# Where a mixer's weights are split, and how the last tile and the norm are cut

## The chip, the cores and the metric

The kernel runs on one core of a Trainium2 chip, in one launch. The metric is the device time of that core in microseconds (us), as a median of several executions. The tables come from one execution that the hardware profiler recorded: its own time, its span (first to last instruction) and, within it, every instruction's start and duration. Engines: PE is TensorE, whose weight loads are shown apart as PEld; DVE is VectorE, ACT ScalarE, POOL GpSimd, SP SyncE, which here only issues DMAs. Each engine works its own list in its own order and waits on semaphores.

## The reference, cut to what matters

One encoder layer on 512 tokens of width 1024, in float32:

```python
def swiglu(x, w_gate, w_up, w_down):
    return (jax.nn.silu(x @ w_gate) * (x @ w_up)) @ w_down

x = x + 0.5 * swiglu(rms_norm(x, ffn1_norm), ffn1_w_gate, ffn1_w_up, ffn1_w_down)   # d_ff = 2816
h = rms_norm(x, mix_norm)
qkv_a, z_a, a_a, b_a, qkv_b = split(h @ w_in)          # w_in: 1024 x 3600
o_a = gdn_mixer(qkv_a, z_a, a_a, b_a, conv_w, ...)     # bidirectional gated DeltaNet, 4 heads of 128
o_b = dilated_mixer(qkv_b, q_norm_w, k_norm_w, rel_bias)   # windowed softmax attention, 8 heads of 64
x = x + concatenate([o_a, o_b]) @ w_out
x = x + 0.5 * swiglu(rms_norm(x, ffn2_norm), ffn2_w_gate, ffn2_w_up, ffn2_w_down)
x = rms_norm(x, final_norm)
```

## The kernel before

Activations lie transposed: eight tiles `x[0..7]` of 128 features x 512 tokens. A product in nearly full precision is made of three matmuls in the reduced type fp32r (`mm3`, line 228): every operand is split into a rounded part `hi` (a cast on ACT) and the remainder `lo` (a subtraction on DVE), and PE sums hi x hi, hi x lo and lo x hi. So weights have to be split on the chip before PE can use them, and each tile of 128x128 weights costs three matmuls of 512 columns.

**First SwiGLU block** (`ffn`, line 284, called with `gu1`, `dn1`). For each of 22 slices of d_ff, gate (`pg`) and up (`pu`) are summed over eight k tiles; then eight output tiles `pd` are summed over the 22 slices. Weights of one such sum come by `wload` (line 165): one DMA on SP's queue into `wraw` (two buffers), a cast into `whi` (line 176), a subtraction into `wlo` (line 177).

**Presplit.** In the same block `share` (line 280) calls `presplit` (line 196) 76 times. It loads one 128x512 piece of weights that come later (56 of `w_in`, 16 of `w_out`, 4 of the second block's first slice, listed in `plan`), casts it into `phi` (line 205), subtracts in place (`praw`, line 206), and `send` (line 191) stores both parts to DRAM (`ws`). All these DMAs are on SP's queue, in program order with the block's own loads.

**Mixer.** A generator per piece of work, and `interleave` (line 63), a planner with hand-set due times, fix the program order; a scheduler places instructions on the engines from it. `px` runs the projections in the order of the string `ORDER`: two *units* of weights for each 128 features (a unit is one piece of `plan`, four 128x128 tiles, 12 matmuls). `wnext` (line 213) hands out a unit: it issues the loads of ready-split units from `ws` (512 KB each) up to `AHEAD` = 3 in advance into the pool `w` of four buffers. Beside the projections run four heads' `gram` (line 594: transposes, products, eight scaled products `M` each on DVE, and eight small `D` stores on SP), `solve` (line 814: 122 small operations on DVE), the levels of a triangular inverse, the `scan`, and attention `att`. In this part PE's order is fixed.

**Second SwiGLU block** (`late=True`): as the first, without presplit; its first slice takes four units from `wnext`. Behind the last output tile (d = 7) stands the final norm: `x[7]` is updated in two halves of 256 tokens (line 335), squared, summed over features by a matmul with ones into `pr`, then `rsq` (line 233) makes the inverse root in `R`, and eight products `y` by `R` (line 1237, two of them on POOL) are stored.

Of the kernel before, what the change touches and what calls it, by code (L numbers as in the profile page):

```python
# [35 lines left out]
GIN, VGO, VGV, PRG, NRG, VTG, VBG, OPG, OTG, FNG, SVG, SSD, SST, VTP, LVH = 9.5, 16.5, 4.0, 0.5, 6.0, 3.5, 3.5, 13.5, 0.75, 10.5, 0.75, 8.0, 0.6, 3.0, 1.3  # L36
AHEAD = 3
PRI = 0, 1, 2, 4, 3, 5
# [52 lines left out]
def encoder_layer(ctx, tc, xT, gu1, dn1, win, wab, wo1, wo2, gu2, dn2, cols, relb, masks, onehot, lnc, sel, out):  # L91
# [95 lines left out]
    plan += [gu2[0, j, :, 4 * u:4 * u + 4] for j in range(2) for u in range(2)]  # L187
    ws_d = [dr.tile([P, 2 * T], F32, name=f"ws{i}") for i in range(len(plan))]
    made, raws, unsent = [0], [], []
# [6 lines left out]
    def presplit():  # L196

        i = made[0]
        made[0] += 1
        for n in range(i if i == 0 else i + 1, min(i + 2, len(plan))):  # L200
            raws.append(tmp("xp", "praw", T + 4, bufs=3)[:, 0:T])
            sy.dma_start(out=raws[-1], in_=plan[n].rearrange("p a b -> p (a b)"))
        lo = raws.pop(0)
        hi = WF["pool"].tile([P, T], F32R, tag="phi", name="phi", bufs=2)
        se.copy(hi, lo)  # L205
        ve.tensor_tensor(out=lo.bitcast(F32R), in0=lo, in1=hi.bitcast(F32), op=ALU.subtract)  # L206
        if unsent:
            send()
        unsent.append((i, hi, lo))

    taken, ready = [0], []

    def wnext():
        while taken[0] < len(plan) and len(ready) <= AHEAD:
            t = wp.tile([P, 1024], F32, tag="w", name="wsp", bufs=4)
            sy.dma_start(out=t, in_=ws_d[taken[0]])
            taken[0] += 1
            ready.append([t[:, i * T:(i + 1) * T].bitcast(F32R).rearrange("p (a b) -> p a b", b=P) for i in range(2)])
        return ready.pop(0)

# [58 lines left out]

    def share(step):  # L280
        while made[0] < len(plan) and made[0] * (2 * NF + 3 * NKT - 8) < len(plan) * (step - 3):
            presplit()

    def ffn(gu, dn, norm, nxt, then=None, late=False, mid=None):
        with tc.tile_pool(name="wf", bufs=2, reuse_waits="tile") as wf, \
# [5 lines left out]
            for f in range(NF):  # L291
                pg, pu = palt("pg"), palt("pu")
                for j, pt in ((0, pg), (1, pu)):
# [27 lines left out]
                wait = []  # L321
            for d in range(NKT):
                pd = palt("pd")
                for f0, n in ((0, 8), (8, 8), (16, 6)):
                    wh, wl = wload(dn[d, :, f0:f0 + n], n, P)
                    if not late:
                        share(2 * NF + 3 * d + f0 // 8)
# [3 lines left out]
                    if late and d == NKT - 1 and f0 == 8:  # L331
                        with tc.issue_after(act["mm"].ins):
                            mid()
                for s in (slice(0, 256), slice(256, 512)) if late and d == NKT - 1 else (slice(0, 512),):
                    ve.scalar_tensor_tensor(out=x[d][:, s], in0=pd[:, s], scalar=0.5, in1=x[d][:, s], op0=ALU.mult,
                                            op1=ALU.add)
                nxt(d)
# [19 lines left out]
    ffn(gu1, dn1, n1, after1, bring)  # L357
    while unsent:
        send()
    with tc.issue_after(act["lastf"].ins):  # L360
        sy.dma_start(out=mk, in_=masks)

    with ExitStack() as mctx:
        mp = mctx.enter_context(tc.tile_pool(name="mp", bufs=1, reuse_waits="tile"))
# [856 lines left out]
    hs = [slice(256 * i, 256 * i + 256) for i in range(2)]
    tail = tmp("sq", "tail")
    preload()
    for pr, s in zip(prs, hs):
        se.activation(tail[:, s], x[7][:, s], AF.Square)
        te.matmul(pr[:, 0:256], lhsT=ones, rhs=tail[:, s], start=False, stop=True)
        rsq(R[:, s], pr[:, 0:256], 1024.0, "u")
    ys.append(slot("xh7", "y"))
    for d in range(NKT):
        y = ys[d]  # L1230
        if d == NKT - 1:
            ve.scalar_tensor_tensor(out=y, in0=x[d], scalar=col[:, C_FIN + d:C_FIN + d + 1], in1=R, op0=ALU.mult,
                                    op1=ALU.mult)
            (sy, se)[d % 2].dma_start(out=out[d], in_=y)
        else:
            for s in hs if d == 0 else (slice(0, T),):
                (gp if d in (1, 4) else ve).tensor_tensor(out=y[:, s], in0=y[:, s], in1=R[:, s], op=ALU.mult)  # L1237
                (sy, se)[d % 2].dma_start(out=out[d, :, s], in_=y[:, s])

# [79 lines left out]
```

## Time and profile before

| what | us |
|---|---|
| median of three executions | 1121.74 (1119.83 to 1124.93) |
| the profiled execution, its own time | 1124.95 |
| its span | 1123.2 |
| busy in the span: PE / PEld | 1071.6 / 871.1 |
| busy in the span: DVE / ACT / POOL | 613.1 / 441.1 / 90.3 |
| mean granted TensorE clock | 0.990 |

Busy times are unions of recorded durations. Matmuls are pipelined and their ends are modelled, so a recorded duration (0.39 us for 512 columns) is longer than the distance from one start to the next, and a PE that is busy is not a PE at its peak. An idle time is put down to the semaphore that came last before the waiting instruction.

### The profile page before, as it was taken

Reading aid. Unit: us, or ns where it says so; the run is one execution under the profiler, and the core shown is the slowest. Engines: PE = TensorE matmul, PEld = TensorE weight load, DVE = VectorE, ACT = ScalarE, POOL = GpSimd, SP = SyncE. Lnnn points to the kernel's source line nnn. Section 1 sums busy time; section 2 is a strip of 40 time slices with the busy share of each in tenths; the row PEclk is TensorE's granted clock in tenths of the full one; section 3 lists DMA queues with packets and bytes.
Section 4 is the critical chain, followed back from the end, with each engine's and each line's share of the span. In section 5 each row is a group of like instructions: output and inputs, shape, how many; then the busy total and the mean of one; then the engine's idle time right before and its main releaser. Section 6 shows DMA issues by size and latency. Waiting matters only on the chain. (4 is left out here: it accounts for less than half of the span.)

```text
span 1123.2 us, 14359 instructions
## 1 busy us (share of the span) xinstructions
PE 1071.6 (95%) x5312; PEld 871.1 (78%) x5312; DVE 613.1 (55%) x1108; ACT 441.1 (39%) x812; POOL 90.3 (8%) x121
## 2 busy tenths in 40 slices
PE   8999999999999999999999989999999999999994
PEld 5787777777788868778788867778888888888883
DVE  5655655655443358678566778565444444522223
ACT  6533443444332226422574756344332222322221
POOL 3000000000011123440000020100000000001111
PEclk9999999999999999999999999999999999999997
DMA  7788888988993334676723363352222323323332
GB/s 258 263 267 281 278 290 285 297 279 278 305 306 120 99 117 158 188 229 217 181 86 99 112 212 111 110 191 93 95 94 94 97 97 107 96 86 101 100 88 75
DMA packets 85062, 191.99 MB, mean 171 GB/s; under 512 B 21520, under 2 KB 22320, under 8 KB 84992
## 3 DMA queue, kind: packets, MB, share of 16 engines
q1 hardware_dynamic: 80800, 178.68, 49.7%
q0 software_dynamic: 2896, 10.25, 3.0%
q10 hardware_dynamic: 1296, 2.15, 0.5%
q8 instruction: 41, 0.67, 0.3%
q14 instruction: 29, 0.24, 0.1%
HBM read 142.24 MB, written 48.81 MB: 170 GB/s over the span
## 5 line engine op out<-in xcount | busy, mean ns | idle before, releaser
L176 ACT CAST whi<-wraw 128x1024 fp32r<-128x1024 f32 (+1 forms) x138 | 137.5, 998 | 269.0 <-PE pd L53 91.3
L177 DVE TENSOR_TENSOR wlo<-wraw,whi 128x1024 fp32r<-128x1024 f32 (+1 forms) x138 | 159.9, 1159 | 107.4 <-ACT whi L176 105.2
L53 PE MATMUL pg<-xh,whi 128*128 128x512 f32 x344 | 136.8, 398 | 7.2 <-ACT whi L176 7.2
L53 PE MATMUL pg<-xh,wlo 128*128 128x512 f32 x344 | 136.5, 397 | 6.9 <-DVE wlo L177 6.9
L53 PE MATMUL pd<-hh,whi 128*128 128x512 f32 x352 | 137.9, 392 | 2.6 <-ACT whi L176 2.6
L53 PE MATMUL pu<-xh,wlo 128*128 128x512 f32 x344 | 134.8, 392 | 4.8 <-DVE wlo L177 4.8
L53 PE MATMUL pd<-hh,wlo 128*128 128x512 f32 x352 | 137.7, 391 | 0.0
L53 PE MATMUL pd<-hl,whi 128*128 128x512 f32 x352 | 137.5, 391 | 0.0
L53 PE MATMUL pg<-xl,whi 128*128 128x512 f32 x344 | 135.9, 395 | 0.1
L53 PE MATMUL pu<-xh,whi 128*128 128x512 f32 x344 | 134.1, 390 | 0.0
L53 PE MATMUL pu<-xl,whi 128*128 128x512 f32 x344 | 133.9, 389 | 0.0
L206 DVE TENSOR_TENSOR praw<-praw,phi 128x512 fp32r<-128x512 f32 x76 | 53.4, 706 | 116.1 <-ACT phi L205 116.0
L205 ACT CAST phi<-praw 128x512 fp32r<-128x512 f32 x76 | 47.0, 620 | 155.7 <-DMA praw<-in_win 103.3
L53 PEld LDWEIGHTS pg<-xh,wlo 128*128 128x128 f32 x344 | 65.3, 190 | 24.8 <-DVE wlo L177 11.3
L53 PEld LDWEIGHTS pg<-xh,whi 128*128 128x128 f32 x344 | 65.3, 190 | 22.5 <-ACT whi L176 8.7
L53 PEld LDWEIGHTS pu<-xh,wlo 128*128 128x128 f32 x344 | 64.5, 188 | 21.5 <-DVE wlo L177 8.4
L53 PEld LDWEIGHTS pd<-hh,whi 128*128 128x128 f32 x352 | 66.5, 189 | 16.7 <-ACT whi L176 3.1
L53 PEld LDWEIGHTS pd<-hh,wlo 128*128 128x128 f32 x352 | 66.3, 188 | 14.7 <-DVE wlo L177 0.9
L53 PEld LDWEIGHTS pg<-xl,whi 128*128 128x128 f32 x344 | 65.1, 189 | 16.1 <-DVE xl L269 2.5
L53 PEld LDWEIGHTS pd<-hl,whi 128*128 128x128 f32 x352 | 66.5, 189 | 14.0
L53 PEld LDWEIGHTS pu<-xl,whi 128*128 128x128 f32 x344 | 64.6, 188 | 13.5
L53 PEld LDWEIGHTS pu<-xh,whi 128*128 128x128 f32 x344 | 64.6, 188 | 13.5 <-ACT whi L176 0.3
(292 smaller groups left out, 1626.9 us busy)
## 6 DMA issues: line engine op xcount, KB each, us to landing
wraw<-in_gu SPq DMA_DIRECT2D x84, 512.0 KB, 3.9
wsp<-ws SPq DMA_DIRECT2D x76, 512.0 KB, 3.5
ws<-phi SPq DMA_DIRECT2D x76, 256.0 KB, 3.6
ws<-praw SPq DMA_DIRECT2D x76, 256.0 KB, 4.5
wraw<-in_dn SPq DMA_DIRECT2D x32, 512.0 KB, 3.6
praw<-in_win SPq DMA_DIRECT2D x56, 256.0 KB, 4.2
wraw<-in_dn SPq DMA_DIRECT2D x16, 384.0 KB, 3.2
praw<-in_wo SPq DMA_DIRECT2D x16, 256.0 KB, 4.1
```

Source lines behind the costliest of these rows:

```text
L53: self.last = f(*a, **k)
L176: se.copy(hi[:, s], raw[:, s])
L177: ve.tensor_tensor(out=lo[:, s], in0=raw[:, s], in1=hi.bitcast(F32)[:, s], op=ALU.subtract)
L205: se.copy(hi, lo)
L206: ve.tensor_tensor(out=lo.bitcast(F32R), in0=lo, in1=hi.bitcast(F32), op=ALU.subtract)
```

## The change

- `presplit`, `send`, `share`, the DRAM tiles `ws` and `AHEAD` are gone. The pool of four weight buffers becomes two tags: `wa` with three and `wb` with one; in the SwiGLU blocks `wtile` hands them out in turn.
- `wopen`, at the end of the first block, takes `wb` as one raw tile `wrw` with two halves and issues two loads. `wnext` keeps up to three `wa` tiles, splits every one but the newest (cast on ACT, subtraction on DVE) and issues the raw load two units ahead into the half that the split has just left.
- The last output tile of the second block is made in two halves of 256 tokens: three `wload`s first, then 66 matmuls of 256 columns for each half. `mid(0)` and `mid(1)` put the ones-matmuls, and the whole final norm of the first half (`close(0)`), into the stream of matmuls; `close(1)` follows the second half. All products and stores have 256 columns now.
- Eight matmuls of ones with ones stand first in PE's list.

```diff
-AHEAD = 3
+    pw = pat("warm")
+    for i in range(8):
+        te.matmul(pw[:, 0:P], lhsT=ones, rhs=ones, start=True, stop=True)
...
-            hi, lo = (wp.tile([P, 1024], F32R, tag="w", name=nm, bufs=4) for nm in ("whi", "wlo"))
+            hi, lo = (wtile(nm) for nm in ("whi", "wlo"))
...
-    def send():
-        i, hi, lo = unsent.pop(0)
-        sy.dma_start(out=ws_d[i][:, 0:T], in_=hi.bitcast(F32))
-        sy.dma_start(out=ws_d[i][:, T:2 * T], in_=lo)
...
+    def wtile(name, dt=F32R):
+
+        nw[0] += 1
+        t, n = ("wb", 1) if nw[0] % 4 == 0 else ("wa", 3)
+        return wp.tile([P, 1024], dt, tag=t, name=name, bufs=n)
+
+    def fetch(i):
+        if i < len(plan):
+            r = wraw[0][:, i % 2 * T:(i % 2 + 1) * T]
+            sy.dma_start(out=r, in_=plan[i].rearrange("p a b -> p (a b)"))
+            fetched.append(r)
+
+    def wopen():
+        while nw[0] % 4 != 3:
+            nw[0] += 1
+        wraw.append(wtile("wrw", F32))
+        for i in range(2):
+            fetch(i)
...
     def wnext():
-        while taken[0] < len(plan) and len(ready) <= AHEAD:
-            t = wp.tile([P, 1024], F32, tag="w", name="wsp", bufs=4)
-            sy.dma_start(out=t, in_=ws_d[taken[0]])
...
+        while got[0] < len(plan) and len(ready) < 3:
+            t = wp.tile([P, 1024], F32R, tag="wa", name="wsp", bufs=3)
+            ready.append(t)
+            got[0] += 1
+        while got[1] < got[0] - (got[0] < len(plan)):
+            i = got[1] - got[0] + len(ready)
+            split(ready[i][:, 0:T], ready[i][:, T:2 * T], fetched.pop(0))
+            got[1] += 1
+            fetch(got[1] + 1)
+        t = ready.pop(0)
...
-                    if not late:
-                        share(2 * f + j)
...
+            if late:
+                d = NKT - 1
+                ws = [wload(dn[d, :, f0:f0 + n], n, P, f0 == 0) for f0, n in ((0, 8), (8, 8), (16, 6))]
+                for i in range(2):
+                    pd, s = palt("pd"), slice(256 * i, 256 * i + 256)
+                    for f in range(NF):
+                        wh, wl = ws[f // 8]
+                        mm3(pd[:, 0:256], wh[:, f % 8], wl[:, f % 8], hh[f][:, s], hl[f][:, s], f == 0, f == NF - 1)
+                        if (i, f) in ((0, 15), (1, 4)):
+                            with tc.issue_after(act["mm"].ins):
+                                mid(i)
...
+    def close(i):
+
+        s, pr = hs[i], prs[i]
+        te.matmul(pr[:, 0:256], lhsT=ones, rhs=n4.tail[:, s], start=False, stop=True)
+        rsq(R[:, s], pr[:, 0:256], 1024.0, "u")
...
+            (se if i and d % 2 else sy).dma_start(out=out[d, :, s], in_=y[:, s])
```

SP's list at the first and the last of the four heads' `D` stores. `wsp<-ws` before and `wrw<-in_win` now are the load of one unit each, `MM` is the solve's input. Before:

```order
L216 DMA wsp<-ws_109 128x1024
L640 DMA D_3160<-M 32x4x32 x8
L216 DMA wsp<-ws_110 128x1024
...
L216 DMA wsp<-ws_118 128x1024
L640 DMA D_3160<-M 32x4x32 x8
L216 DMA wsp<-ws_119 128x1024
L820 DMA MM<-D_3160 64x1024 x2
```

And now:

```order
L201 DMA wrw<-in_win 128x512 x12
L644 DMA D_2564<-M 32x4x32 x8
L201 DMA wrw<-in_win 128x512 x6
...
L644 DMA D_2564<-M 32x4x32 x8
L201 DMA wrw<-in_win 128x512 x2
L824 DMA MM<-D_2564 64x1024 x2
```

The stores stand between the same kind of loads, but the load behind them is of a unit that comes two units after the last one split, where it was three or four units in advance.

DVE's list at the first head's gram (`xp` and `z` are what leaves PSUM for a projection, `qT<-xp,col,qT` a tap of the short convolution). Before:

```order
L424 TENSOR_TENSOR xp<-pc,R 128x512
L551 TENSOR_TENSOR gb<-mk,gh 128x512
L430 SCALAR_TENSOR_TENSOR qT<-xp,col,qT 128x512
L551 TENSOR_TENSOR gb<-mk,gl 128x512
L430 SCALAR_TENSOR_TENSOR qT<-xp,col,qT 128x512 x2
...
L629 TENSOR_TENSOR itr<-pkq,mk 128x512
L613 TENSOR_TENSOR c_3156<-beta,n2k 128x2x4
L629 TENSOR_TENSOR itr<-pkq,mk 128x4x128
L615 TENSOR_TENSOR bdec<-c_3156,cs 128x2x4
L634 SCALAR_TENSOR_TENSOR M<-pkk,c_3156,M 128x128 x8
L424 TENSOR_TENSOR xp<-pc,R 128x512
```

And now:

```order
L226 TENSOR_TENSOR wsp<-wrw,wsp 128x512
L434 SCALAR_TENSOR_TENSOR qT<-xp,col,qT 128x512
L555 TENSOR_TENSOR gb<-mk,gl 128x512
L434 SCALAR_TENSOR_TENSOR qT<-xp,col,qT 128x512 x2
...
L633 TENSOR_TENSOR itr<-pkq,mk 128x512
L617 TENSOR_TENSOR c_2560<-beta,n2k 128x2x4
L633 TENSOR_TENSOR itr<-pkq,mk 128x4x128
L619 TENSOR_TENSOR bdec<-c_2560,cs 128x2x4
L638 SCALAR_TENSOR_TENSOR M<-pkk,c_2560,M 128x128 x8
L226 TENSOR_TENSOR wsp<-wrw,wsp 128x512
```

The first and the last of these rows are the remainders of two units that follow each other; the second one stands behind the gram's work.

DVE's list in the solve (`stp` and `ZZ` are its small operations). Now:

```order
L835 TENSOR_TENSOR stp<-ZZ,MM 128x115
L428 TENSOR_TENSOR xp<-pc,R 128x512
L839 TENSOR_TENSOR ZZ<-ZZ,stp 128x5x23
L226 TENSOR_TENSOR wsp<-wrw,wsp 128x512
L835 TENSOR_TENSOR stp<-ZZ,MM 128x110 x2
L839 TENSOR_TENSOR ZZ<-ZZ,stp 128x5x22 x2
L835 TENSOR_TENSOR stp<-ZZ,MM 128x126
L835 TENSOR_TENSOR stp<-ZZ,MM 128x105
L839 TENSOR_TENSOR ZZ<-ZZ,stp 128x6x21
L839 TENSOR_TENSOR ZZ<-ZZ,stp 128x5x21
L226 TENSOR_TENSOR wsp<-wrw,wsp 128x512
```

Before, the same list has the solve's operations and one `xp` there and no `wsp`; now a unit's remainder stands behind every eight or so of them.

## Rows read from the trace of the kernel before

**Rows 1.** Stages: us, busy (xcount) by engine PE to POOL, clock, DMA, GB/s.

```profile
14.17:396.11 381.94, 365.65 (x1566) 293.48 (x1564) 199.93 (x249) 151.59 (x216) 23.05 (x24) 0.99 0.78 256
410.87:548.16 137.29, 132.10 (x685) 107.09 (x684) 105.92 (x314) 55.92 (x159) 35.20 (x54) 1.00 0.66 196
548.16:745.91 197.75, 187.03 (x1384) 156.43 (x1381) 136.41 (x336) 105.12 (x268) 14.35 (x21) 0.99 0.39 131
745.91:1108.05 362.14, 362.10 (x1593) 298.54 (x1591) 149.35 (x175) 112.12 (x141) 10.17 (x6) 1.00 0.31 95
```

**Rows 2.** Chain of waits in order of time, second block: start, duration, what.

```profile
775.24 5.44 PE pu L53 x24
```

**Rows 3.** Waits of PE, 14.17 to 396.11: total us, times, longest.

```profile
PE pg L53 <- DVE wlo L177: 6.9, 8, 1.2
PE pu L53 <- DVE wlo L177: 4.8, 8, 1.5
PE pd L53 <- ACT whi L176: 2.6, 1, 2.6
PE pg L53 <- ACT whi L176: 1.9, 2, 1.1
```

**Rows 4.** Waits of SP's DMA queue, 14.17 to 396.11.

```profile
SPq L193 <- ACT phi L205: 92.1, 37, 4.5
```

**Rows 5.** Stages, the solve and the stretch before it.

```profile
473.56:500.73 27.17, 25.51 (x128) 20.85 (x126) 19.36 (x53) 8.13 (x28) 15.48 (x20) 1.00 0.67 204
500.73:528.53 27.80, 27.80 (x125) 23.03 (x125) 27.80 (x133) 3.88 (x9) 0.52 (x1) 1.00 0.68 214
```

**Rows 6.** Timeline of the end: start, duration, instruction.

```profile
1107.62 0.39 PE L53 MATMUL pd<-hh,wlo 128*128 128x512 f32 x1
...
1118.95 0.34 ACTq L1234 DMA_DIRECT2D out_y<-y  x1
```

**Rows 7.** The page's groups: busy us, mean ns | idle before, releaser.

```profile
L206 DVE TENSOR_TENSOR praw<-praw,phi 128x512 fp32r<-128x512 f32 x76 | 53.4, 706 | 116.1 <-ACT phi L205 116.0
L205 ACT CAST phi<-praw 128x512 fp32r<-128x512 f32 x76 | 47.0, 620 | 155.7 <-DMA praw<-in_win 103.3
```

**Rows 8.** DMA issues, second block: count, KB each, median us to landing.

```profile
wraw<-in_gu SPq DMA_DIRECT2D x38, 512.0 KB, 3.5
...
wraw<-in_dn SPq DMA_DIRECT2D x8, 384.0 KB, 3.2
```

**Rows 9.** DMA issues, 400 to 550.

```profile
wsp<-ws SPq DMA_DIRECT2D x42, 512.0 KB, 4.3
```

**Rows 10.** Groups by line on DVE, dense projections.

```profile
L430 DVE SCALAR_TENSOR_TENSOR vT<-xp,col,vT 128x512 f32<-128x512 f32 x16 | 11.9, 745 | 1.9 <-ACT vT L426 1.7
...
L634 DVE SCALAR_TENSOR_TENSOR M<-pkk,c,M 128x128 f32<-128x128 f32 x32 | 9.0, 343 | 6.3 <-POOL itr L631 6.3
```

**Rows 11.** Timeline of PE at the first head's gram.

```profile
443.89 0.60 PE L51 MATMUL ptk<-mk,kT 128*128 128x128 f32 x4
...
446.18 1.06 PE L51 MATMUL pkq<-qT,kT 128*128 128x128 f32 x8
```

**Rows 12.** Timeline of SP's queue at the first D stores.

```profile
451.28 4.69 SPq L640 DMA_DIRECT2D D<-M  x8
```

**Rows 13.** Timeline of PE in the out-projection, matmuls of 256 columns.

```profile
718.50 1.19 PE L51 MATMUL pov<-PT,vb 128*128 128x256 f32 x8
719.53 0.39 PE L51 MATMUL pd<-goh,wsp 128*128 128x512 f32 x1
```

**Rows 14.** Groups by line behind the last matmul.

```profile
L1237 DVE TENSOR_TENSOR y<-y,R 128x512 f32<-128x512 f32 (+1 forms) x6 | 5.3, 946 | 0.0
...
L162 ACT ACTIVATE R<-pr,eps 128x256 f32<-128x256 f32 x2 | 0.9, 474 | 0.5 <-PE pr L53 0.5
```

**Rows 15.** DMA issues behind 1100.

```profile
out_y<-y SPq DMA_DIRECT2D x2, 128.0 KB, 1.9
```

**Rows 16.** Timeline of the first projection: the last tile.

```profile
13.60 0.19 PEld L53 LDWEIGHTS pg<-xl,whi 128*128 128x128 f32 x1 [0.50 <-DVE xl L269]
```

More of the change, by code (lines that the diff above doesn't have):

```diff
@@ L187, in encoder_layer @@
     plan += [gu2[0, j, :, 4 * u:4 * u + 4] for j in range(2) for u in range(2)]
-    ws_d = [dr.tile([P, 2 * T], F32, name=f"ws{i}") for i in range(len(plan))]
-    made, raws, unsent = [0], [], []
-    def send():
-        i, hi, lo = unsent.pop(0)
-        sy.dma_start(out=ws_d[i][:, 0:T], in_=hi.bitcast(F32))
-        sy.dma_start(out=ws_d[i][:, T:2 * T], in_=lo)
[L196 to L209, printed above, removed]
@@ L211, in encoder_layer @@
-    taken, ready = [0], []
-    def wnext():
-        while taken[0] < len(plan) and len(ready) <= AHEAD:
-            t = wp.tile([P, 1024], F32, tag="w", name="wsp", bufs=4)
-            sy.dma_start(out=t, in_=ws_d[taken[0]])
-            taken[0] += 1
-            ready.append([t[:, i * T:(i + 1) * T].bitcast(F32R).rearrange("p (a b) -> p a b", b=P) for i in range(2)])
-        return ready.pop(0)
+    nw, got, fetched, ready, wraw = [0], [0, 0], [], [], []
+    def wtile(name, dt=F32R):
+        nw[0] += 1
+        t, n = ("wb", 1) if nw[0] % 4 == 0 else ("wa", 3)
+        return wp.tile([P, 1024], dt, tag=t, name=name, bufs=n)
@@ new lines, in fetch @@
+    def fetch(i):
[9 more added lines that the diff above has]
+            fetch(i)
+    def wnext():
+        while got[0] < len(plan) and len(ready) < 3:
[8 more added lines that the diff above has]
+        t = ready.pop(0)
+        return [t[:, i * T:(i + 1) * T].rearrange("p (a b) -> p a b", b=P) for i in range(2)]
@@ L278, in rstd @@
             rsq(R, pr, 1024.0)
-    def share(step):
-        while made[0] < len(plan) and made[0] * (2 * NF + 3 * NKT - 8) < len(plan) * (step - 3):
-            presplit()
     def ffn(gu, dn, norm, nxt, then=None, late=False, mid=None):
@@ L321, in ffn @@
                 wait = []
-            for d in range(NKT):
+            for d in range(NKT - 1 if late else NKT):
                 pd = palt("pd")
@@ L325, in ffn @@
                     wh, wl = wload(dn[d, :, f0:f0 + n], n, P)
-                    if not late:
-                        share(2 * NF + 3 * d + f0 // 8)
                     for i in range(n):
@@ L330, in ffn @@
                         mm3(pd, wh[:, i], wl[:, i], hh[f], hl[f], f == 0, f == NF - 1)
[L331 to L335, printed above, removed]
+                ve.scalar_tensor_tensor(out=x[d], in0=pd, scalar=0.5, in1=x[d], op0=ALU.mult, op1=ALU.add)
+                nxt(d)
+            if late:
[9 more added lines that the diff above has]
+                                mid(i)
+                    ve.scalar_tensor_tensor(out=x[d][:, s], in0=pd[:, 0:256], scalar=0.5, in1=x[d][:, s], op0=ALU.mult,
                                             op1=ALU.add)
@@ L357, in encoder_layer @@
     ffn(gu1, dn1, n1, after1, bring)
-    while unsent:
-        send()
     with tc.issue_after(act["lastf"].ins):
         sy.dma_start(out=mk, in_=masks)
+    wopen()
     with ExitStack() as mctx:
@@ L1214, in last @@
             se.mul(ys[d], x[d], col[:, C_FIN + d:C_FIN + d + 1])
-    def mid():
-        for i, pr in enumerate(prs):
-            te.matmul(pr[:, 0:256], lhsT=ones, rhs=n4.acc[:, 256 * i:256 * i + 256], start=True, stop=False)
-    ffn(gu2, dn2, n3, last, late=True, mid=mid)
[L1221 to L1238, printed above, removed]
+    hs = [slice(256 * i, 256 * i + 256) for i in range(2)]
@@ new lines, in close @@
+    def close(i):
+        s, pr = hs[i], prs[i]
+        te.matmul(pr[:, 0:256], lhsT=ones, rhs=n4.tail[:, s], start=False, stop=True)
+        rsq(R[:, s], pr[:, 0:256], 1024.0, "u")
+        for d in range(NKT):
+            y = ys[d]
+            if d == NKT - 1:
+                ve.scalar_tensor_tensor(out=y[:, s], in0=x[d][:, s], scalar=col[:, C_FIN + d:C_FIN + d + 1], in1=R[:, s],
+                                        op0=ALU.mult, op1=ALU.mult)
+            else:
+                (gp if d in (1, 4) else ve).tensor_tensor(out=y[:, s], in0=y[:, s], in1=R[:, s], op=ALU.mult)
+            (se if i and d % 2 else sy).dma_start(out=out[d, :, s], in_=y[:, s])
@@ new lines, in mid @@
+    def mid(i):
+        if i == 0:
+            for pr, s in zip(prs, hs):
+                te.matmul(pr[:, 0:256], lhsT=ones, rhs=n4.acc[:, s], start=True, stop=False)
+            ys.append(slot("xh7", "y"))
+            n4.tail = tmp("sq", "tail")
+            preload()
+        else:
+            se.activation(n4.tail[:, hs[0]], x[7][:, hs[0]], AF.Square)
+            close(0)
+    ffn(gu2, dn2, n3, last, late=True, mid=mid)
+    se.activation(n4.tail[:, hs[1]], x[7][:, hs[1]], AF.Square)
@@ L1241, in _bucket @@
+    close(1)
 def _bucket(rel):
```

## The prediction, made before the changed kernel ran

> **What bounds the kernel now.** I read the stage table first [rows 1]. The second SwiGLU block (745.91 to 1108.05 on the span's clock) is the yardstick: PE is busy 362.10 of 362.14 us, and the chain of waits shows 24 matmuls in 5.44 us, so 0.2267 us each [rows 2]. The first SwiGLU block has the same 1,584 matmuls, of which 24 are over at 14.17. The other 1,560 need 1,560 x 0.2267 = 353.6 us, and the norm's ones-matmuls 1.7, together 355.4; the stage took 381.94. So 26.6 us of it are lost. The waits of PE in this stage name only two releasers, `whi` and `wlo` of line 176 and 177 [rows 3]: 6.9 + 4.8 + 2.6 + 1.9 = 16.2 us. The rest is the restart after each gap and the half clock (granted mean 0.99). The splits themselves are short; what is late is the raw weight load, for SP's queue stands still in front of it: its stores of `phi`, which are the presplit's, wait 92.1 us in 37 places for the cast [rows 4]. DMA is at 0.78 there and at 0.31 in the second block.
>
> In the mixer I took two stages, the dense projections (410.87 to 548.16, weight units 3 to 41; a unit is four 128x128 tiles of weights, 12 matmuls, 2.72 us) and the stretch where attention and scan share PE with the other 34 units (548.16 to 745.91). PE is at 132.10 of 137.29 and 187.03 of 197.75. DVE has 105.92 and 136.41: no longer a spare engine, and in the solve (500.73 to 528.53) it is busy 27.80 of 27.80 us [rows 5]. At the end, 15.2 us of the span lie behind the last matmul [rows 6].
>
> **The change part by part.** *Presplit out of the first block.* 76 casts of 620 ns, 76 subtractions of 706 ns [rows 7] and 228 DMAs of 256 KB go, with SP's waits. The second block, with the same code and no presplit, shows no stall; what is late next there is nothing. Two raw loads and three splits of the mixer are put at the end of the stage; an ACT cast may stand some 3 us for its load, beside down weights that are split a unit (5.44 us) ahead. I take -26 us; bounds -26.6 and -10 (only the clock and the longest waits go).
>
> *Splits into the mixer.* 73 casts and 73 subtractions at the same 620 and 706 ns, each now ahead of the matmuls of its unit. Before, a unit came ready-made by DMA with up to four buffers. Now a split can start when the unit three back is done, so PE can be at most two units (5.44 us) ahead; and the raw tile has two halves, so a load waits for the split two back. That loop is issue 0.34 + landing + 0.62 + 0.71. The landing of a 256 KB load in the mixer isn't shown. In the second block 384 KB take 3.2 and 512 KB 3.5 us, which by line gives an estimate of 2.9 for 256; in the dense stage 512 KB took 4.3, the upper bound [rows 8, 9]. I take 3.2, nearer to the first, since the change halves these bytes. 4.9 us for two units against 5.44: it holds, with 0.5 us for both queues. Where it breaks:
>
> (a) The four heads' grams. The order shows between two splits four taps (0.75 us each), eight M products (0.343 each) and three more of 128x512, priced as taps: 3.0 + 2.7 + 2.3, with the split 8.7 us, and 6.3 us of DVE's waits for POOL over the four heads come on top [rows 10]. PE has 5.44 of lead and the gram's own matmuls (443.89 to 447.24, less a wait and a projection's matmuls between: 2.6) [rows 11]: short by up to 2.3. At the same place SP issues eight `D` stores in 4.69 us [rows 12], now with a raw load right behind: 4.69 + 0.34 + 3.2 + 0.62 + 0.71 = 9.6 us against 8.0. I take 2.5 us per head, 10 in all; bounds 0 (lead covers it) and 20 (both add up, after each head).
>
> (b) The solve. DVE is full for 27.8 us in which PE uses ten units; ten subtractions add 7.1. The lead takes up to 5.4 of them; what DVE has free afterwards comes too late for a PE that is held to two units. 1.7 to 7.1; I take 4.
>
> (c) Units 42 to 75. PE does other work between them, so a split is seldom what PE waits for, but it stands in the queues in which the score and scan chains pass. At worst 34 x 0.71 = 24 us, at best 0; I take 4, nearer to nothing since a unit there comes every 5.8 us.
>
> Together +18, bounds +2 and +51.
>
> *Last tile by halves.* PE: 66 matmuls of 512 columns (15.0 us) become 132 of 256. Eight such matmuls took 718.50 to 719.53, 0.129 us each, though four of them have 64-column weights [rows 13]. 132 x 0.129 = 17.0; half of 0.2267 gives 15.0; one weight load in the open each, 0.19, gives 25.1. With 0.4 for one more ones-matmul I take +1, bounds 0 and +10. Rows show the load of a 512 matmul hidden: 0.2267 is 512 columns at 2.4 GHz (0.213) and little else. The Trainium skill's page "TensorE: Matmul & The Clock Gate" gives a load P/1.2 ns (section "LDWEIGHTS (loading the stationary operand)"), 107 ns for 128 columns, and says in "The mechanism" that loads overlap matmuls only in another row group. By that second rule the halves would add 66 more open loads, 7 us, an estimate from that page; [rows 2] speaks against it, for at 512 columns it would be 0.32 and not 0.2267 each.
>
> After the last matmul one half of 256 columns is left: update of x, square, ones-matmul, three steps of ACT and two of DVE, eight at up to 0.474: 3.9 with the hand-overs. Then six products of DVE at half of 0.946, 2.8. Issue 0.34, landing 1.9, end 0.3: 9.2 against 15.2 [rows 6, 14, 15]. The first half's chain (3.9 + 2.8 = 6.7 us) lies beside 66 matmuls, 8 us. -6; with PE -5, bounds -6.5 and +4.
>
> *Ones-matmuls at first.* The first 24 matmuls end at 14.17, since each waits for its x and split: the last still waited 0.50 for `xl` [rows 16]. A faster PE gains nothing there; if the eight are not over at 5.3 they cost up to 2. I take 0.
>
> **Sum.** -26 + 18 - 5 = -13 against the profiled 1124.95 (span 1123.2 and 1.75 around): 1112. The median, 1121.74, lies 3.2 lower; by it 1109. I write 1110.
>
> **The rivals,** from 1122 as a base. *DVE and the raw loop pace the projections.* If the landing stays at 4.3 and a split waits 0.8 us in each queue, the loop is 0.34 + 4.3 + 0.62 + 0.71 + 1.6 = 7.6 us for two units, 3.8 each against 2.72 (the point is 5.44). Over 39 units that is +42, with (c) and the tail 1122 - 26 - 5 + 46 = 1137. For it: DVE at 27.80 of 27.80 and the 4.3 under load. Against: DMA is then lighter. 0.14.
> *The splits vanish in the gaps.* DVE has 31 us free in the dense stage, 61 in the next; if the order keeps each split two units ahead, the mixer costs 4: 1122 - 26 - 5 + 4 = 1095. Against: its idle time stands at other places than its peaks. 0.15.
> *Give and take.* The mixer costs 26 to 36: 1117 to 1127. 0.15.
> *The first block keeps its stalls* (they come from two raw buffers, not from SP): -8, with +18 and -5 it is 1127 and above. Against: the second block has the same buffers and no stall. 0.04.
> *Open weight loads in the last tile:* +7 to +10 on the forecast, 1119. 0.02.
>
> **How the numbers follow.** The forecast has 0.50 with its own range 1100 to 1117. Measurement can tell 0.5% (5.6 us) from no change: below 1116.1 is faster, above 1127.3 slower. Faster: 0.50 and 0.15, and 0.02 of the give and take, 0.67. Slower: 0.14 and 0.03. Same: the rest, 0.16. The range leaves out some 0.08 below 1097 and 0.13 above 1128.
>
> **What would show it.** The stage up to the mixer about 369 us long (356 from 14.17), no wait of PE for `whi` or `wlo` in it, DMA near 0.35 and SP's waits for `phi` gone. In the mixer PE's waits for DVE line 226 (the subtraction of `wsp`), largest behind the `D` stores and in the solve, some 14 us in the dense stage; DVE there at 130 or so. The end 9 to 10 us behind the last matmul, and 256-column matmuls at 0.12 to 0.13. I am wrong if the waits for line 226 pass 25 us, if they stay under 5, or if the first block keeps more than 5 us of stalls.

## The result and the profile after

The changed kernel takes 1110.68 us as a median of four executions (1109.03 to 1113.57), the kernel before, run beside it, 1123.34 (1119.83 to 1127.42): ratio 0.9889, interval 0.9846 to 0.9932. The profiled execution has a span of 1107.8 us against 1123.2. The forecast was 1110, from a sum of -13 us; the spans differ by 15.4.

The same cuts as before, read from both traces (first matmul of `pu`, first matmul with `wsp`, first matmul of the second block, end of the last `pd`, end of the span):

| stage | before | after | difference | forecast |
|---|---|---|---|---|
| up to the first `pu` matmul | 14.17 | 13.74 | -0.4 | 0 |
| rest of the first block | 381.94 | 355.68 | -26.3 | -26 |
| mixer | 349.80 | 364.36 | +14.6 | +18 |
| second block | 362.1 | 363.5 | +1.4 | +1 |
| behind its last matmul | 15.2 | 10.5 | -4.7 | -6 |
| span | 1123.2 | 1107.8 | -15.4 | -13 |

The stage rows of the changed kernel (us, busy time of PE, PEld, DVE, ACT, POOL with counts, granted clock, DMA share, GB/s), which answer to [rows 1]: first block, dense projections, the rest of the mixer, second block.

```profile
13.74:369.42 355.68, 355.68 (x1566) 293.43 (x1565) 156.37 (x176) 112.13 (x143) 20.30 (x15) 1.00 0.33 105
384.18:536.11 151.93, 138.78 (x685) 110.93 (x684) 131.53 (x355) 77.85 (x197) 34.96 (x54) 0.96 0.43 114
536.11:733.78 197.67, 185.74 (x1384) 155.19 (x1381) 152.40 (x363) 121.69 (x298) 11.92 (x21) 1.00 0.28 87
733.78:1097.30 363.52, 363.42 (x1661) 302.56 (x1659) 155.35 (x188) 114.92 (x147) 11.57 (x8) 1.00 0.30 95
```

The first block is now full of matmuls from end to end at the full clock, with DMA at 0.33 where it had 0.78, and no wait of PE is left in it, where [rows 3] had 16.2 us. The dense stage has grown from 137.3 to 151.9 us, and its clock is 0.96: all of the mixer's cost is there (the next stage takes 197.7 as before).

PE's waits in the dense stage (total us, times, longest):

```profile
PE ptv L50 <- ACT vtok L700: 3.6, 1, 3.6
PE pkq L50 <- DVE M L638: 3.5, 1, 3.5
PE pdc L50 <- ACT gb L561: 2.9, 1, 2.9
PE pc L50 <- DVE wsp L226: 1.2, 1, 1.2
```

The subtraction of the weights (`wsp`, line 226) holds PE up for 1.2 us in all. The three long waits are for other things: `vtok` (0.8 before), `M` (1.7 before) and `gb` (0.5 before). Behind each the granted clock falls to the lower of its two levels for a while: behind the wait for `M` matmuls of 512 columns start 0.43 us apart (453.63, 454.06, 454.49) and not 0.23. Ten-microsecond windows around the three:

```profile
410.00:420.00 10.00, 8.07 (x28) 6.52 (x29) 7.53 (x11) 7.63 (x20) 1.35 (x4) 0.83 0.18 52
450.00:460.00 10.00, 7.28 (x29) 6.01 (x30) 7.96 (x21) 1.91 (x5) 6.79 (x8) 0.83 0.42 116
520.00:530.00 10.00, 5.92 (x25) 4.47 (x24) 5.21 (x8) 7.73 (x18) 0.00 (x0) 0.77 1.07 185
530.00:540.00 10.00, 10.00 (x151) 8.16 (x150) 7.17 (x12) 5.09 (x11) 0.00 (x0) 0.88 0.36 69
```

Over the whole mixer PE stands idle for 25.1 us against 15.9, +9.2, and is busy 5.4 us longer for the same 2,130 matmuls (339.28 against 333.89): together the 14.6. (The three waits are 10.0 us long in all, where they were 3.0.)

Why `vtok` comes late is seen in ACT's timeline (start, duration, instruction, in brackets the idle time before and what ended it):

```profile
521.78 0.62 ACT L229 CAST wsp<-wrw 128x512 fp32r<-128x512 f32 x1 [3.73 <-DMA wrw<-in_win]
522.30 0.62 ACT L153 ACTIVATE vT<-vT 128x512 f32<-128x512 f32 x1
522.95 1.28 ACT L159 ACT_TABLE_LOAD   x1
...
526.26 1.65 ACT L700 ACTIVATE vtok<-ptr,ivn 128x128 f32<-128x128 f32 x6
```

and in PE's:

```profile
527.19 1.11 PE L50 MATMUL ptv<-mk,vbT 128*128 128x128 f32 x4 [3.55 <-ACT vtok L700]
```

The cast of a weight unit has waited 3.73 us for its raw load. Behind it, in ACT's order, stand the last Silu, the table load and the copies into `vtok` that the transposes need. Before, that table load began at 532.82 and `vtok` at 540.44, 7.6 us apart; here it is in the way. Over the mixer the casts of `wsp` wait like this for two things, the load and PE's release of the tile:

```profile
ACT wsp L229 <- PE pc L50: 21.9, 12, 5.3
ACT wsp L229 <- DMA wrw<-in_win: 21.5, 16, 3.7
...
ACT wsp L229 <- PE pd L50: 10.5, 8, 2.4
```

The raw load itself is no slower than assumed (median 2.7 us from issue to landing, where I took 3.2 between the bounds of [rows 8, 9]):

```profile
wrw<-in_win SPq DMA_DIRECT2D x42, 256.0 KB, 2.7
```

The last tile: the first matmuls of 256 columns, with the last of 512 ahead of them,

```profile
1079.73 0.40 PE L52 MATMUL pd<-hh,wlo 128*128 128x512 f32 x1
1079.97 0.28 PE L52 MATMUL pd<-hh,whi 128*128 128x256 f32 x1
1080.09 0.28 PE L52 MATMUL pd<-hl,whi 128*128 128x256 f32 x1
1080.21 0.28 PE L52 MATMUL pd<-hh,wlo 128*128 128x256 f32 x1
```

0.12 us each, as [rows 13] had it and without an open load. The chain of waits at the end (start, duration, what):

```profile
1094.97 2.29 PE pd L52 x19
...
1097.28 0.43 DVE x L340
...
1098.21 0.71 PE pr L52 x2
...
1100.80 0.44 DVE R L245
...
1101.26 0.43 DVE y L1233
...
1104.08 0.40 DVE y L1230
```

From the end of the last matmul (1097.28) to `R` (1101.24) 3.96 us, to the last product (1104.48) 3.24, and 3.3 until the span ends.

### The profile page after: what moved, and what is told of

It is laid out like the page before. It is cut to its first block, busy times and chain, and to the rows that moved or that the text cites. A ratio compares the mean times of both kernels' runs of the same rounds, so it can differ in the third digit from the quotient of the medians.

```text
span 1107.8 us, 14127 instructions
## 1 busy us (share of the span) xinstructions
PE 1071.4 (97%) x5394; PEld 881.4 (80%) x5394; DVE 614.7 (55%) x1113; ACT 443.6 (40%) x812; POOL 86.6 (8%) x123
## 4 chain that ended last, share of the span: by engine, by line
PE 82%; DVE 9%; ACT 3%; issue 3%; DMA 2%; POOL 1%; DVEq 0%; SPq 0%; ACTq 0%; POOLq 0%
PE pg L52 22%; PE pd L52 22%; PE pu L52 22%; PE pc L50 3%; PE pd L50 2%; PE pqk L50 2%; PE ps L50 2%; PE pl L50 1%; DVE wsp L226 1%; PE pout L52 1%; DMA wrw<-in_win 1%; PE pT L50 1%; PE pvb L50 1%; PE pov L50 1%; PE pS L50 1%
## 5 line engine op out<-in xcount | busy, mean ns | idle before, releaser
L52 PE MATMUL pd<-hh,whi 128*128 128x512 f32 (+1 forms) x374 | 141.2, 378 | 0.0
L52 PE MATMUL pd<-hh,wlo 128*128 128x512 f32 (+1 forms) x374 | 140.9, 377 | 0.0
L52 PE MATMUL pd<-hl,whi 128*128 128x512 f32 (+1 forms) x374 | 140.8, 377 | 0.0
L316 DVE TENSOR_TENSOR u<-pu,R 128x512 f32<-128x512 f32 x44 | 30.4, 691 | 129.6 <-PE pu L52 129.6
L52 PEld LDWEIGHTS pd<-hh,whi 128*128 128x128 f32 x374 | 70.3, 188 | 13.0
L52 PEld LDWEIGHTS pd<-hh,wlo 128*128 128x128 f32 x374 | 70.3, 188 | 13.0
L52 PEld LDWEIGHTS pd<-hl,whi 128*128 128x128 f32 x374 | 70.3, 188 | 12.9
L229 ACT CAST wsp<-wrw 128x512 fp32r<-128x512 f32 x76 | 47.3, 622 | 76.9 <-DMA wrw<-in_win 24.0
L314 DVE TENSOR_TENSOR g<-pg,R 128x512 f32<-128x512 f32 x44 | 30.4, 691 | 84.7 <-PE pg L52 84.7
L52 PEld LDWEIGHTS pg<-xh,whi 128*128 128x128 f32 x344 | 65.0, 189 | 14.9 <-ACT whi L178 1.3
L52 PEld LDWEIGHTS pg<-xh,wlo 128*128 128x128 f32 x344 | 64.9, 189 | 13.9 <-DVE wlo L179 0.3
```

The costliest lines, as they stand in the source:

```text
L52: self.last = f(*a, **k)
L314: ve.tensor_tensor(out=g, in0=pg, in1=R, op=ALU.mult)
L316: ve.tensor_tensor(out=u, in0=pu, in1=R, op=ALU.mult)
```

## The experiments

Stage times of all runs, with the same cuts (us):

| run | first block | mixer | second block | behind it | span |
|---|---|---|---|---|---|
| before | 381.9 | 349.8 | 362.1 | 15.2 | 1123.2 |
| changed | 355.7 | 364.4 | 363.5 | 10.5 | 1107.8 |
| f_stores_pool | 438.1 | 347.8 | 362.1 | 15.8 | 1177.2 |
| f_all_pool | 435.8 | 348.9 | 362.3 | 14.9 | 1180.2 |
| d_dma | 369.6 | 366.0 | 363.4 | 10.5 | 1123.2 |
| d_comp | 356.7 | 364.3 | 363.8 | 10.5 | 1108.6 |
| m_cast_pool | 355.4 | 374.0 | 363.7 | 10.3 | 1117.3 |
| m_sub_pool | 355.4 | 383.9 | 364.4 | 10.2 | 1128.2 |
| m_noload | 355.4 | 355.9 | 363.4 | 10.8 | 1099.6 |
| m_noload4 | 355.6 | 358.5 | 363.2 | 10.8 | 1101.8 |
| t_alone | 378.8 | 348.6 | 363.4 | 10.5 | 1115.3 |
| h_pre46 | 370.8 | 354.2 | 363.6 | 10.1 | 1112.1 |
| h_paced46b | 357.4 | 348.7 | 363.4 | 10.1 | 1093.5 |
| t_paced76b | 365.0 | 348.2 | 363.4 | 10.5 | 1100.8 |

### What the presplit cost in the first block

**f_stores_pool** (the first two lines) and **f_all_pool** (all three): the kernel before, with other queues.

```diff
-        sy.dma_start(out=ws_d[i][:, 0:T], in_=hi.bitcast(F32))
-        sy.dma_start(out=ws_d[i][:, T:2 * T], in_=lo)
+        gp.dma_start(out=ws_d[i][:, 0:T], in_=hi.bitcast(F32))
+        gp.dma_start(out=ws_d[i][:, T:2 * T], in_=lo)
...
-            sy.dma_start(out=raws[-1], in_=plan[n].rearrange("p a b -> p (a b)"))
+            gp.dma_start(out=raws[-1], in_=plan[n].rearrange("p a b -> p (a b)"))
```

> The kernel before, its presplit kept whole, but the 152 stores of the split weights are issued by POOL's DMA queue and not by SP's. Theory 1 (SP's queue: raw weight loads stand behind stores that wait for a cast, 92.1 us of waits in the kernel before): the first block loses little, its stretch from 13.7 or 14.2 us to the mixer takes 355 to 362 us where it took 381.94, and the run is 20 to 26 us shorter, 1097 to 1103. Theory 2 (the DMA engines, 0.78 busy there, or the memory are what makes the loads late): the same bytes move, so the stretch stays above 375 us and the run above 1115. Theory 3 (ACT's list: the cast of a weight that PE needs stands behind a presplit's cast that waits for its own raw load): part comes back, 362 to 375 us, and PE waits for whi and wlo stay.

> The kernel before with all 228 DMAs of the presplit, its raw loads too, on POOL's queue. Theory 1 (SP's queue): like the stores alone, 355 to 360 us for the first block's stretch and 1097 to 1101 for the run. Theory 2 (DMA load): above 375 us and 1115. Theory 3 (ACT's list): no better than the stores alone, since the raw loads of the presplit would then stand behind the stores' waits on POOL and the casts on ACT would wait longer: 365 to 380 us.

Measured: 1178.66 us (1.0464 times before, 1.0430 to 1.0498) and 1180.45 (1.0494, 1.0458 to 1.0529). Theory 1, mine from the prediction, fails: with the stores out of SP's queue the block loses 82 us and not 26, with the raw loads out too 80. Theory 2's times (above 375 us and 1115) are met, but the same bytes do not explain that the loss rises; theory 3's ranges are missed. The waits of PE in f_stores_pool, and the landing of the block's raw loads up to 300 us:

```profile
PE pg L53 <- ACT whi L176: 22.0, 9, 4.8
PE pu L53 <- ACT whi L176: 14.7, 8, 4.6
PE pu L53 <- DVE wlo L177: 11.6, 13, 1.5
PE pg L53 <- DVE wlo L177: 4.2, 7, 0.9
```

```profile
wraw<-in_gu SPq DMA_DIRECT2D x38, 512.0 KB, 5.4
```

5.4 us, where it is 4.9 in the kernel before over the same 300 us and 3.4 in the changed kernel. The Trainium skill's page "DMA: Bandwidth & Descriptors" says in "Queues, rings and completion order" that a DMA engine serves the queue rows that have work in turn. No run here shows these turns: in d_dma, below, the same loads take 5.8 us with SP's queue alone.

But the loads are not what PE waits for. In f_stores_pool 36 of PE's 37 waits for `whi` or `wlo` (47.8 of 52.6 us) are for a weight whose cast `whi` began right behind a presplit's cast `phi` in ACT's list, some 4 us or more after its raw load had landed. In f_all_pool, where SP's queue has none of the presplit's DMAs, it is 35 of 38 (42.9 of 45.0 us). It is so in the kernel before as well: 17 of its 19 waits (13.9 of 16.2 us), with the load there 1.2 to 2.4 us before the cast, once 9.6. One of them, whose raw load was issued at 106.00 and landed at 110.69:

```profile
106.00 0.42 SPq L175 DMA_DIRECT2D wraw<-in_gu  x1
111.42 0.62 ACT L205 CAST phi<-praw 128x512 fp32r<-128x512 f32 x1 [4.86 <-DMA praw<-in_win]
...
112.47 0.62 ACT L205 CAST phi<-praw 128x512 fp32r<-128x512 f32 x1
112.99 1.05 ACT L176 CAST whi<-wraw 128x1024 fp32r<-128x1024 f32 x1
115.76 0.50 PE L53 MATMUL pg<-xh,wlo 128*128 128x512 f32 x1 [0.94 <-DVE wlo L177]
```

A `phi` waits 4.86 us for its own raw load, and what the block needs stands behind it. That is theory 3's wait, if not its size. SP's waits also held the presplit back: up to 300 us ACT's list has 70 `phi` beside 48 `whi` in the kernel before, and 76 beside 38 in f_stores_pool.

**d_dma** and **d_comp**: the changed kernel with one half of the presplit put back, in the same places.

```diff
+    def presplit():     # d_dma; raws: 256 KB loads on SP, one ahead
...
+        lo = raws.pop(0)
+        sy.dma_start(out=ws_d[i][:, 0:T], in_=lo)
+        sy.dma_start(out=ws_d[i][:, T:2 * T], in_=lo)
+    def presplit():     # d_comp
...
+        se.copy(hi, x[7])
+        ve.tensor_tensor(out=lo.bitcast(F32R), in0=x[7], in1=hi.bitcast(F32), op=ALU.subtract)
```

> The changed kernel with the presplit's DMAs alone put back into the first block: 76 raw loads and 152 stores of 256 KB on SP's queue, paced as before; no cast and no subtraction, and nobody reads what is stored. The stores wait for the load they store, not for a cast. The stretch from 13.74 us to the mixer takes 355.7 us in the changed kernel and took 381.9 before. Theory A (bytes: 58 MB more on DMA engines that are then 0.8 busy make the raw weight loads late): 370 us or more, with waits of PE for whi and wlo. Theory B (the presplit's casts and subtractions, waiting in ACT's and DVE's lists ahead of the block's own): below 358 us, no such wait. Theory C (SP's queue held up by stores that wait for a cast): below 362 us, since these waits are shorter.

> The changed kernel with the presplit's casts and subtractions alone put back into the first block (76 of each, from a tile of x that is there already); no DMA and nobody reads them. Theory A (bytes) and theory C (SP's queue): nothing moves, 355.5 to 356.5 us from 13.74 us to the mixer. Theory B (ACT's and DVE's lists): 362 us or more.

Measured, one execution each: 1125.02 and 1110.36 us. The first block's windows, of d_dma while its presplit lasts and after it, then of d_comp:

```profile
13.74:240.00 226.26, 223.24 (x971) 181.27 (x970) 104.83 (x125) 70.75 (x92) 8.67 (x6) 1.00 0.92 313
240.00:383.33 143.33, 137.68 (x595) 112.02 (x595) 52.00 (x52) 39.92 (x51) 11.74 (x15) 0.99 0.56 181
```

```profile
13.23:369.97 356.74, 355.81 (x1565) 293.39 (x1564) 201.68 (x252) 154.22 (x219) 23.48 (x24) 1.00 0.33 105
```

The work alone costs 1.1 us (theories A and C had up to 0.8, theory B 6 or more). But the casts of d_comp wait for nothing, so it says nothing of a cast that waits in ACT's list. The DMAs alone cost 13.9 of the 26.3, 0.4 less than theory A's 370 and more than theory C's 362. They do it by another wait than in the kernel before: no `phi` stands in ACT's list, the raw loads take 5.8 us, and in 7 of 10 waits the cast begins 0.1 us or less behind its load. The other 11.3 us come only with both, casts that wait for loads and stores that wait for casts; these two runs do not part them.

**h_pre46**, **h_paced46b**, **t_paced76b**: fewer units split early, and split in another place. In h_pre46 the first 46 units come from the presplit of the kernel before into four buffers, and the raw tile is opened behind them. The other two have the lower hunks as well, in `presplit` (t_paced76b on t_alone).

```diff
+            if got[0] < NPRE:
+                g, n = ("wb", 1) if got[0] % 4 == 3 else ("wa", 3)
+                t = wp.tile([P, 1024], F32, tag=g, name="wsp", bufs=n)
+                sy.dma_start(out=t, in_=ws_d[got[0]])
...
-            sy.dma_start(out=raws[-1], in_=plan[n].rearrange("p a b -> p (a b)"))
+            with tc.issue_after(act["lastf"].ins):
+                sy.dma_start(out=raws[-1], in_=plan[n].rearrange("p a b -> p (a b)"))
...
-            send()
+            with tc.issue_after(act["lastf"].ins):
+                send()
```

> Of the 76 units the first 46 are split in the first block and stored as in the kernel before (SP's queue, same pacing, so 0.6 of the presplit per us), and come ready-made into four buffers; the other 30 are split in the mixer as in the changed kernel. Last tile and first matmuls as in the changed kernel. Theory A (bytes: 34 MB of the block's own and 35 MB, 195 GB/s against the 256 to 290 at which loads were late): the first block's stretch takes 356 to 361 us. Theory B or C (each presplit costs its share of the 26 us): 369 to 374 us. The mixer loses no more than 4 us to splits in either (units 44 to 75 lost nothing in the changed kernel), 350 to 354 us, so the run is 1094 to 1101 by theory A, 1105 to 1113 by the others.

> The kernel with 46 units split in the first block, but each of the presplit's loads and stores is placed behind the latest raw weight load of the block in SP's list, one unit a step; without this SP's list has about three units for every two of the block's loads, and they were all done at 225 us while the block lost 15 us. Theory P (the presplit costs only because it runs ahead at all the DMA gives, 256 to 290 GB/s, and stands in front of the block's loads): the first block's stretch takes 356 to 361 us and not 370.8, the mixer 354 us as there, the run 1095 to 1102. Theory Q (each presplit costs its 0.33 us wherever it stands): 368 to 373 us and 1109 to 1114.

> The kernel before with the last tile by halves and the ones-matmuls, all 76 units split in the first block, and the presplit's loads and stores placed behind the block's latest raw load in SP's list. 92 MB in 355 us are 260 GB/s, so there is little to spare. Theory P: 357 to 368 us for the stretch that takes 378.8 without the placing, the run 1098 to 1109. Theory Q: 376 to 382 us, the run 1115 to 1121.

Measured: 1111.39 us (0.9872 of before, 0.9849 to 0.9896), 1096.02 (0.9758, 0.9735 to 0.9781) and 1102.83 (0.9823, 0.9791 to 0.9856). Without the new place, 46 units cost 15.1 us of the first block, 0.33 each, as 76 had cost 26.3, 0.35 each; theory A's 356 to 361 is refuted. With it they cost 1.7, and 76 cost 9.3 in place of 23.1 (t_alone): the times of theory P. The first block of h_pre46 up to 225 us and behind it, then that of h_paced46b:

```profile
13.42:225.00 211.58, 201.67 (x863) 160.01 (x862) 120.86 (x158) 90.22 (x130) 10.77 (x12) 1.00 0.80 262
225.00:384.19 159.19, 159.19 (x703) 131.79 (x702) 60.87 (x61) 44.62 (x56) 12.73 (x12) 1.00 0.37 117
```

```profile
13.74:371.16 357.42, 356.20 (x1566) 293.24 (x1565) 185.03 (x219) 138.25 (x186) 21.57 (x24) 1.00 0.63 208
```

h_pre46 is through with its presplit at 225 us and loses all it loses until then; h_paced46b moves the same bytes over the whole block, at 208 GB/s. So an early split costs by where it stands, more than by its bytes. But the new place in SP's list moved ACT's list too: in h_pre46 the 46 `phi` stand among 31 `whi`, 27 of them right behind a `phi`; in h_paced46b among 57, and 6 are. Whether the loads' place or the casts' does it, these runs do not part; the waits shown above speak for the casts'. h_paced46b is also the fastest version: its dense stage gets ready-made units as before and loses nothing (mixer 348.7 us), and the later units are split in the mixer, where the changed kernel lost nothing either. Its span is 14.3 us shorter than the changed kernel's (1093.5 and 1107.8). The mixers of h_pre46 and h_paced46b have the same program and take 354.2 and 348.7 us, where 350 to 354 and 354 were expected; that difference, of one execution each, stays unexplained.

### What the splits cost in the mixer

**m_cast_pool** and **m_sub_pool**: one half of a unit's split moved to POOL.

```diff
-            split(ready[i][:, 0:T], ready[i][:, T:2 * T], fetched.pop(0))
+            raw = fetched.pop(0)
+            gp.tensor_copy(out=ready[i][:, 0:T], in_=raw)                 # m_cast_pool
+            sub(ready[i][:, T:2 * T], raw, ready[i][:, 0:T])
+            se.copy(ready[i][:, 0:T], raw)                                # m_sub_pool
+            gp.tensor_tensor(out=ready[i][:, T:2 * T], in0=raw, in1=ready[i][:, 0:T].bitcast(F32), op=ALU.subtract)
```

> The changed kernel, but in the mixer the casts of the units (76, ACT line 229) are made by POOL; the subtractions stay on DVE. The mixer is 369.42 to 733.78 there, 364.4 us, 14.6 more than before. Theory 1 (ACT's list: a cast that waits for its raw load, 21.5 us in 16 places, or for a unit tile that PE still reads, holds up the small ACT operations behind it that the grams and the values need; PE's three longest waits, for gb 2.9, M 3.5 and vtok 3.6 us, come from there, and the half clock behind each costs as much again): these three waits go below 1 us each, the mixer takes 351 to 356 us and the run is 8 to 13 us shorter than the changed kernel. Theory 2 (DVE: 52 us of subtractions in a list that is full in the solve): nothing moves, 361 to 367 us. Theory 3 (the raw loop: two raw halves are too few): the slower cast makes the loop longer, PE waits for the subtraction (line 226 or the like) by over 5 us, and the mixer takes 367 us or more.

> The changed kernel, but in the mixer the 76 subtractions of the units are made by POOL (a 128x512 product takes 1.3 us there against 0.7 on DVE); the casts stay on ACT. Theory 1 (ACT's list): the three waits for gb, M and vtok stay, the mixer takes 362 to 372 us, the run is the same as the changed kernel or up to 8 us slower. Theory 2 (DVE): DVE is 52 us lighter and the mixer takes 351 to 356 us, the run 8 to 13 us shorter. Theory 3 (the raw loop): the loop is longer by 0.6 us and more, PE waits for the subtraction, 367 us or more.

Measured: 1119.06 us (0.9955 of before, 0.9938 to 0.9973) and 1131.20 (1.0058, 1.0040 to 1.0076), 8 and 20 us above the changed kernel. Theories 1 and 2 fail: neither ACT nor DVE made lighter helps. Theory 3 has the side right (over 367 us), but not the wait: PE waits 2.5 and 1.8 us for the subtraction, not over 5. DVE's timeline of m_cast_pool at the second gram shows why the wait for `M` stayed at 3.5 us:

```profile
445.44 0.69 DVE L228 TENSOR_TENSOR wsp<-wrw,wsp 128x512 fp32r<-128x512 f32 x1 [1.39 <-POOL wsp L220]
446.04 0.16 DVE L616 TENSOR_SCALAR wk<-wk 128x4 f32<-128x4 f32 x1
```

ACT's part of the gram was ready earlier now, but DVE stood in front of `wk`, its next step, with a subtraction that waited 1.39 us for a cast, on POOL. The wait had moved from one list to another. The work grew too: on POOL a cast takes 0.76 us and a subtraction 1.46.

**m_noload** (first hunk) and **m_noload4** (the others): the splits without what they wait for.

```diff
-            sy.dma_start(out=r, in_=plan[i].rearrange("p a b -> p (a b)"))
+            if i < 2:                                                     # m_noload
+                sy.dma_start(out=r, in_=plan[i].rearrange("p a b -> p (a b)"))
...
-            fetched.append(r)
+            fetched.append(mk[:, 0:T])
...
-        while got[0] < len(plan) and len(ready) < 3:
-            t = wp.tile([P, 1024], F32R, tag="wa", name="wsp", bufs=3)
+        while got[0] < len(plan) and len(ready) < 4:
+            g, n = ("wb", 1) if got[0] % 4 == 3 else ("wa", 3)
+            t = wp.tile([P, 1024], F32R, tag=g, name="wsp", bufs=n)
```

> The changed kernel with the raw loads of the mixer left out after the first two (every unit is split from the same two raw halves, so the product isn't the reference's); casts, subtractions and the three unit tiles stay. The mixer takes 364.4 us in the changed kernel and took 349.8 before. Theory W (a split that waits in an in-order list holds up what stands behind it, the gram's and the values' small operations; here it waits for its raw load or for PE to release the tile): the gap in front of vtok, whose cast waited 3.7 us for a load, goes with its half clock, some 6 us, those at the grams stay: 356 to 360 us. Theory V (the 100 us of casts and subtractions themselves, as work on ACT and DVE): 362 to 366 us.

> As the kernel without raw loads, but every unit is split from a constant that lies in SBUF, and the raw tile is a fourth unit tile, so a split waits neither for a load nor, as a rule, for PE to release a tile; the work of casts and subtractions is the same, and they may run three units ahead. Theory W (waiting splits): all three gaps shrink, the mixer takes 350 to 355 us. Theory V (work on ACT and DVE): 361 to 366 us as in the changed kernel.

Measured, one execution each: 1101.39 and 1103.59 us; the mixer takes 355.9 and 358.5. Without loads to wait for, 8.5 of the 14.6 us are gone with the same casts and subtractions: theory W in size. By the starts of the units the place of `vtok` costs 1.7 us in place of 5.9, and the grams, which W said would stay, 2.7 in place of 7.2. PE's longest waits in the dense stage of m_noload:

```profile
PE pdc L50 <- ACT gb L562: 2.9, 1, 2.9
PE ptv L50 <- ACT vtok L701: 2.5, 1, 2.5
PE pkq L50 <- DVE M L639: 1.8, 1, 1.8
```

`M` is back at 1.8 (1.7 before), which W had put down to tiles not released; `vtok` still waits 2.5. m_noload4 is 2.7 us slower than m_noload, outside W's 350 to 355. It was meant to take the wait for tiles away as well, but did not: over the mixer its casts wait some 54 us for PE to release a tile, where it is 60 in m_noload and 43 in the changed kernel. So the remaining 6 us are not taken apart. At `gb` it is the order that was built. ACT's timeline of the changed kernel at the first gram, and of the kernel before:

```profile
404.63 0.40 ACT L561 ACTIVATE gb<-mk,gh 128x128 fp32r<-128x128 f32 x1
...
406.04 1.28 ACT L153 ACT_TABLE_LOAD   x1
...
408.50 1.28 ACT L164 ACT_TABLE_LOAD   x1
...
410.90 0.97 ACT L561 ACTIVATE gb<-mk,gh 128x128 fp32r<-128x128 f32 x3
```

```profile
425.77 1.28 ACT L557 ACTIVATE gb<-mk,gh 128x128 fp32r<-128x128 f32 x4
...
432.44 1.28 ACT L151 ACT_TABLE_LOAD   x1
...
434.90 1.28 ACT L162 ACT_TABLE_LOAD   x1
```

Before, all four copies into `gb` stood ahead of the two table loads; now one does and three stand behind them. m_noload has the same order and the same 2.9 us. No run here restores the old order alone, so how much of the 6 us it is, and how much the wait for tiles, stays open.

### The end

**t_alone**: the kernel before with the edits of the last tile, the norm and the first matmuls alone (the hunks of the change's diff that stand there).

> The kernel before with only the last tile and norm by token halves and the ones-matmuls at first. By the stage tables of the two kernels: start -0.4 us, second block +1.4, behind the last matmul -4.6, so the span is 3.3 to 4.0 us shorter (1119 to 1120). If the gain of the end came from the weight tiles' new pool instead (wa and wb), it is within 1 us of the kernel before.

Measured: 1118.67 us, ratio 0.9951 (0.9931 to 0.9971). Second block +1.3, behind it -4.7, first matmuls -0.1: -3.5 us by the stages concerned, as expected, in the old weight pool. The span fell by 7.9, since the first block came out 3.1 shorter here and the mixer 1.2: that is within the spread of its executions (1115.89 to 1123.55; the medians differ by 5.3).

## Why the prediction was right, and where it was not

*First block, -26: right in size, wrong in its cause.* The yardstick (355.4 without stalls) was met to 0.3 us. But the sentence that what is late is the raw weight load, because SP's queue stands still in front of it for the stores' waits, does not hold. Taking those stores off the queue tripled the loss (f_stores_pool), and at 17 of PE's 19 waits in the kernel before the raw load had landed. In its place the traces show the block's casts behind the presplit's in ACT's list, which wait for their own loads. The runs add that the work alone costs 1.1 us and the DMAs alone 13.9; none changes ACT's list alone, so its share of the 26.3 is not measured.

*Mixer, +18: right in size within its bounds, wrong in the wait it named.* I had PE wait for line 226 by some 14 us and said that under 5 would refute me; it is 1.2. A split did not come too late for PE. It stood, waiting, ahead of small operations that PE needed sooner; without the waits for loads 8.5 of the 14.6 us go, and the rest is not taken apart. By place: grams +7.2 (up to unit 29; I had +10), solve +1.5 (+4), units 42 to 75 -0.1 (+4), and the values' `vtok` +5.9, which I had not at all. The lower clock behind three gaps, 5.4 us, was in no term either. The loop of the raw loads held, as worked out, and DVE is at 131.5 us in the dense stage, as forecast.

*Second block, +1: right.* 1.4, at 0.12 us a matmul. If every load of a 256-column matmul stood in the open, by the rule of the Trainium skill's page "TensorE: Matmul & The Clock Gate" ("LDWEIGHTS (loading the stationary operand)" and "The mechanism") weighed in the prediction, it would be 0.21, an estimate from that page; the trace decides against it. The Trainium skill's page also names, in the same section "The mechanism", loads that go ahead into a background weight buffer; with that the 0.12 agrees.

*Behind the last matmul, -6: mis-sized by 1.3.* The chain to `R` took 3.96 (3.9 forecast), the products 3.24 (2.8: two of the six took 0.94 us each, beside POOL's two products, and not 0.47), issue, landing and end 3.3 (2.54: the span ends 1.3 us behind the last landing and not 0.3, while the 1.9 from issue to landing held the issue's 0.34 already).

*First matmuls, 0: right.* With them the first `pu` matmul starts at 13.2 to 14.2 us in all runs that have them, without at 14.17 in the kernel before and 13.43 in f_stores_pool.

The errors of the mixer (-3.4) and of the end (+1.3) have opposite signs, and the sum is off by 2.4 us between the spans; that the stated 1110 lies within 1 us of the median is partly luck. Of the rivals, the raw loop and DVE as a bound are refuted by line 226's 1.2 us, the vanishing splits by the 14.6, and the first block that keeps its stalls by its missing waits.

## What to carry to other kernels

Work moved into an engine's list costs by what stands behind it while it waits, not by its own duration: look for the operations with a short deadline behind each new waiter. Here that held twice, for the units' splits in the mixer and for the presplit's casts in the first block. When PE waits for a cast, look whether its load had landed before blaming the load. A gap on PE also costs in clock: three of about 3 us came here with 5.4 us of slower matmuls. A prefetch that isn't needed yet did best behind the loads that are, in the same queue, spread over the whole block. And a stage with the same code and no stalls is a yardstick for size, even where the cause is misread.

## What the hardware showed that I had not expected

- The same 152 stores issued from POOL's queue and not SP's raised the loss of the first block from 26 to 82 us; the granted clock up to 300 us fell to 0.92.
- The DMA engines moved 313 GB/s at a share of 0.92 in d_dma up to 240 us while PE lost little (223.24 of 226.26 us busy), so the 256 to 281 GB/s of the kernel before was no ceiling.
- Three gaps of about 3 us in the mixer, 10.0 us where there had been 3.0, came with 5.4 us more of matmul time over the mixer, at the lower of the clock's two levels behind them.
- Two products of 256 columns on DVE took 0.94 us each while POOL made its own two, where the others of that form took 0.41 to 0.43.
